# Five PSUM banks, VectorE scaling and ten constant products at the beginning of a two-layer trunk

## The chip, the core and the metric

The kernel runs on one NeuronCore of a Trainium2 chip. The metric is the device time of one execution in microseconds (us); lower is better. The core has TensorE (matrix products, with results in eight PSUM banks of 128 x 512 float32), VectorE, ScalarE and GpSimd for element-wise work, and SyncE, which issues the transfers between DRAM and SBUF. Each engine works through its own queue in order, and engines wait for each other by semaphores.

## What is computed

The reference is a trunk of two layers over a sequence of 1024 frames of 1024 channels. Layer 0 mixes in time by RWKV-7, layer 1 by a diagonal complex state space (S5). A squared-ReLU MLP follows each mixer, and a layer norm follows each of the four parts. The change touches the first part, the projections of the RWKV mixer:

```python
def rwkv7_time_mix(x, mu, w0, w1, w2, a0, a1, a2, g1, g2, k_k, k_a, r_k,
                   wr, wk, wv, wo, lnx_g, lnx_b):
    xx = jnp.pad(x, ((0, 0), (1, 0), (0, 0)))[:, :-1] - x
    xr = x + xx * mu[0]
    xw = x + xx * mu[1]
    xk = x + xx * mu[2]
    xv = x + xx * mu[3]
    xa = x + xx * mu[4]
    xg = x + xx * mu[5]
    r = xr @ wr
    w_pre = (w0 + jnp.tanh(xw @ w1) @ w2).astype(f32)
    decay = jnp.exp(-jnp.exp(-jax.nn.softplus(-w_pre) - 0.5))
    k = xk @ wk
    v = xv @ wv
    a = jax.nn.sigmoid(a0 + (xa @ a1) @ a2)
    g = jax.nn.sigmoid(xg @ g1) @ g2
    ...
    _, o = lax.scan(step, s0, seq_in)
    ...
    return (o.astype(x.dtype) * g) @ wo
```

## The kernel before

Channels lie on the 128 partitions in 8 tiles (KT = 8), frames along the free axis in two halves of 512 (H = 0 and 1). A product in near-float32 precision is made of three fast passes: `split` (L191, L192) lets ScalarE cast a tile to a high part and VectorE subtract it, which gives the low part; `mm3` then issues high x high, high x low and low x high (`mmb`, L256). A product over all 1024 channels is thus 24 matmuls into one PSUM bank.

`rwkv_proj(0)` computes the projections of the first half. It loads the eight `xs` tiles, with the first two weight tiles of `wa1` (list `first`) behind the first of them (L330, L322). `xo` are the split `xs` tiles; `xm` are the mixed ones for `wk` (`mixes(2)`), whose instructions are ranked early (MIXR = 100). The small projections do not mix the input. `scaled` (L383 on) multiplies the weights by `mu` or `1 - mu` instead, on GpSimd (L389), each half of the tile's 128 columns by its own vector; it splits them and takes the product with `xo`. `shifted` adds the two products, one of them a frame later. So come, in program order: `shifted("wa1")` and `gate_a` (two banks each), `gate_c` (one bank for the product with `g1c`, copied out at L427, and one for the products with the constant `pick`, L429 and L430). Then `rates(n)` (two banks, evicted at L467) and `square("wk", ...)` (one bank, evicted at L493) alternate for n = 0 to 3, and four `square("wr", ...)` follow. There the generator yields for the first time.

Every dense product asks `psd()` for its bank, which goes in turn through the list `banks[0]`. That list is `narrow`, three times the pool `pd`, which has three banks. The other PSUM pools are `pl` (one bank), `pa` (two, for the recurrence) and `pc` (two, tag "c"). `kbtrans` of the recurrence writes its transposes into `pc` (L689).

`core` (L870) takes the first step of `rwkv_proj(0)`, then issues `elem(0)`, which reads the stored projections back (`lda`, `ldsg`, `ldk`, `ldr`, L589) and prepares the first unit of the recurrence, `amat` and `invert`, and then the rest of the projections at the lowest urgency. Eight units of the recurrence follow, with the second half's projections among them. The program order isn't the order on the engines: a planner sorts each engine's instructions ahead of time by rank and by estimated times, and assigns the buffers of the pools; at run time each queue is fixed.

Of the kernel before, what the change touches and what calls it, by code (L numbers as in the profile page):

```python
# [30 lines left out]
LNG = (1, 3, 5)  # L31
LNT = (2, 5)
TB = 2
LN2R = 99000
PAUSE = 8
PRE = 6
# [43 lines left out]
def trunk(ctx, tc, A):  # L80
    nc = tc.nc
    V, S, G, PE, SP = nc.vector, nc.scalar, nc.gpsimd, nc.tensor, nc.sync
# [9 lines left out]
    pc = ctx.enter_context(tc.tile_pool(name="pc", bufs=2, space=PSUM))  # L92

    @contextmanager
    def rank(base):

        keep = tc.cur_priority
        tc.cur_priority = base
        yield
        tc.cur_priority = keep  # L100
# [5 lines left out]
    ident = cp.tile([128, 128], F32, name="ident")  # L106
# [83 lines left out]
    def split(src, hi, lo, e=None):  # L190
        S.copy(hi, src)  # L191
        op = (e or V).tensor_sub(lo, src, hi.bitcast(F32))  # L192
        if e is None or e is V:
            behind(op)
            weave(op, pace_[0])
# [62 lines left out]
    def mm3(p, whi, wlo, xh, xl, first, last):  # L258
        mmb(p, whi, xh, start=first, stop=False)
        mmb(p, whi, xl, start=False, stop=False)  # L260
        mmb(p, wlo, xh, start=False, stop=last)
# [33 lines left out]
    narrow = [(pd, "d")] * 3  # L295
    wide = narrow + [(pa, "a")] * 2 + [(pc, "c")] * 2
    banks, nb = [narrow], [0]

    def psd():
        pool, tag = banks[0][nb[0] % len(banks[0])]  # L300
        nb[0] += 1
        return pool.tile([128, HT], F32, tag=tag, name="d")
# [13 lines left out]
    def rwkv_proj(H):  # L316
# [3 lines left out]
        def wraw(nm, k0):  # L320
            w = wp.tile([128, 4, 128], F32, tag="wraw", name="wsc", bufs=4)
            SP.dma_start(w, A[nm][:, k0 : k0 + 4])  # L322
            return w

        first = []
        for k in range(KT):
            t = ap.tile([128, HT + 1], F32, tag="xs", name="xs", bufs=8)
            if H == 0:
                V.memset(t[:, 0:1], 0.0)
                SP.dma_start(t[:, 1:], A["xT"][k * 128 : (k + 1) * 128, 0:HT])  # L330
                if k == 0:
                    first = [wraw("wa1", k0) for k0 in (0, 4)]
# [49 lines left out]
        def scaled(nm, parts):  # L382
            p = psd()  # L383
            n = 128 // len(parts)
            for k0 in range(0, KT, 4):
                w = first.pop(0) if first else wraw(nm, k0)
                for q, m in enumerate(parts):
                    wq = w[:, :, q * n : q * n + n]
                    G.tensor_mul(wq, wq, m[:, k0 : k0 + 4].unsqueeze(2).broadcast_to([128, 4, n]))  # L389
                hi = wp.tile([128, 4, 128], F32R, tag="whi", name="whi")  # L390
                lo = wp.tile([128, 4, 128], F32R, tag="wlo", name="wlo")
                split(w, hi, lo)
                for k in range(4):
                    mm3(p, hi[:, k], lo[:, k], xo[k0 + k][0], xo[k0 + k][1], k0 + k == 0, k0 + k == KT - 1)
            return p
# [262 lines left out]
    def amat(D):  # L658

        shp = [128, 2, NC, NP, 2, L]  # L660
        if D.m in (1, 3, 5):
            at = ap.tile(shp, F32, tag="q", name="AT2", bufs=1)
        else:
            at = kp.tile(shp, F32, tag="AT", name="AT", bufs=1)
        D.at = at
        for j in range(2):
            for c2 in range(2):
                pp = [pa.tile([128, 2, 2, 128], F32, tag="a", name="pA") for h in range(2)]
                prods = []
                for cc in range(2):  # L670
                    for i in range(2):
                        for h in (1, 0):
                            hs = slice(64 * h, 64 * h + 64)
                            u = 4 * i + 2 * c2 + cc
                            prods.append(PE.matmul(pp[h][:, cc, i], D.KB[j][hs, u].rearrange("p j l -> p (j l)"),
                                                   D.AR[j][hs, u].rearrange("p j l -> p (j l)"), start=True, stop=True))
                inorder(prods)
                for h in range(2):
                    V.tensor_mul(at[:, h, 2 * c2 : 2 * c2 + 2, 2 * j : 2 * j + 2].rearrange("p c i j l -> p c i (j l)"),
                                 pp[h], amask.rearrange("p u j l -> p u (j l)").unsqueeze(1).broadcast_to([128, 2, 2, 128]))  # L680

    def kbtrans(D):
        D.kbt = {}
        for j in range(2):
            for c2 in range(2):
                p = pc.tile([128, 2, 2, 128], F32, tag="c", name="pT")
                for cc in range(2):
                    for i in range(2):
                        PE.transpose(p[:, cc, i], D.KB[j][:, 4 * i + 2 * c2 + cc].rearrange("p j l -> p (j l)"), ident)  # L689
                t = kp.tile([128, 2, 2, 128], F32, tag="kbt", name="kbt", bufs=KTB)  # L690
                S.copy(t, p)
                D.kbt[j, c2] = t
# [171 lines left out]
    def run(gen):  # L864
        for _ in gen:
            pass
# [3 lines left out]
    def core():  # L870

        pg = rwkv_proj(0)
        next(pg)
        bulk.clear()
        with rank(3000):
            cur = elem(0)
        with rank(5000):
            amat(cur)
            invert(cur)
        with rank(100000):  # L880
            run(pg)
        last = None
        for m in range(8):
            if m == PB:
                with rank(100000):
                    run(rwkv_proj(1))
            if m == W0B:

                with rank(WO0R):
                    first_out.append(wo(0))  # L890
                with rank(LN1R):
                    first_out.append(layer_norm(first_out[0], 0, 0, True, True))
            base = m * 10000
            with rank(base + RK[0]):
                kbtrans(cur)
            nxt = None
            if m < 7:
                with rank(base + RK[1]):
                    nxt = elem(m + 1)
            if last and m in GB:  # L900
                with rank(base + RK[2]):
                    gnorm(last, 1)
            with rank(base):
                chain(cur, 0)
            if last and m not in GB:
                with rank(base + RK[2]):
                    gnorm(last, 1)
            if nxt and m < 6:
                with rank(base + RK[3]):
                    amat(nxt)  # L910
            with rank(base + RK[4]):
                chain(cur, 1)
            with rank(base + RK[5]):
                gnorm(cur, 0)
            if nxt:
                with rank(base + RK[6]):
                    if m == 6:
                        amat(nxt)
                    invert(nxt)
            last, cur = cur, nxt  # L920
        with rank(base + 8000):
            gnorm(last, 1)
# [40 lines left out]
    def layer_norm(h, gi, H, split_out=True, by_pe=False):  # L963
        ops = []
        for _ in norm_steps(h, gi, H, split_out, ops, by_pe):
            pass
        return ops
# [136 lines left out]
    def wo(H):  # L1104
        t0 = H * HT
        ys = yload(H)
        hs = []
        for n in range(KT):
            p = psd()
            dense(p, wload(A["wo"][n], KT, 128), ys)  # L1110
            h = htile(H)
            SP.dma_start(h, A["xT"][n * 128 : (n + 1) * 128, t0 : t0 + HT])
            V.scalar_tensor_tensor(h, h, ALPHA, p, op0=ALU.mult, op1=ALU.add)
            hs.append(h)
        return hs
# [463 lines left out]
    def store(H, h):  # L1579
        for k in range(KT):  # L1580
            S.dma_start(A["out"][k * 128 : (k + 1) * 128, H * HT : (H + 1) * HT], h[k])

    core()
    kctx.close()
    sp = ctx.enter_context(tc.tile_pool(name="sp", bufs=1))
# [6 lines left out]
    def first_steps(steps, base):  # L1592
        with rank(base):
            next(steps)
            woven.append([steps, tc.cur_priority])
# [46 lines left out]
    def first_half():  # L1642
        yield from norm_steps(hA, 2, 0, True, xo)
        for k in range(4):
            t = jp.tile([128, HT], F32, tag="ql", name="t1r", bufs=6)
            S.copy(t, hA[k])
            t1.append(t)
            t = jp.tile([128, HT], F32, tag="qh", name="t3r", bufs=6)
            G.tensor_sub(t, hA[k + 4], hA[k])
            t3.append(t)  # L1650
            d = [jp.tile([128, HT], F32R, tag="t1", name="t3", bufs=8) for _ in range(2)]
            split(t, *d)
            tops[2].append(d)
            yield 1

    first_steps(first_half(), LN2R)
    glu(hB, ys)
# [49 lines left out]
    for c in range(2):  # L1707
        db(tuple(range(JB - TB, JB)), False, slice(256 * c, 256 * c + 256), keep)
        if c == 0:
# [77 lines left out]
```

## Time and profile before

| | |
|---|---|
| median of 3 runs | 2559.0 us (2554.05 to 2559.45) |
| profiled execution | 2551.81 us |
| its span in the trace | 2550.0 us |
| instructions | 42959 |
| mean granted TensorE clock | 0.973 |

The trace holds one execution. "Busy" is the time in which an engine had an instruction in work, so the overlapping matmuls make TensorE's figure generous. A row of the timeline has start, duration, engine, line, operation, output and inputs, shapes and count. In brackets stands how long the engine was idle before, and what ended that. A row of the waits has the total, the number and the longest. A row of the stretches has, for each engine, busy time and instructions, then the clock granted to TensorE, the mean share of the 16 DMA engines, and GB/s.

### The profile page before, as it was taken

Reading aid. Unit: us, or ns where it says so; the run is one execution under the profiler, and the core shown is the slowest. Engines: PE = TensorE matmul, PEld = TensorE weight load, DVE = VectorE, ACT = ScalarE, POOL = GpSimd, SP = SyncE. Lnnn points to the kernel's source line nnn. Section 1 sums busy time; section 2 is a strip of 40 time slices with the busy share of each in tenths; the row PEclk is TensorE's granted clock in tenths of the full one; section 3 lists DMA queues with packets and bytes.
Section 4 is the critical chain, followed back from the end, with each engine's and each line's share of the span. In section 5 each row is a group of like instructions: output and inputs, shape, how many; then the busy total and the mean of one; then the engine's idle time right before and its main releaser. Section 6 shows DMA issues by size and latency. Waiting matters only on the chain.

```text
span 2550.0 us, 42959 instructions
## 1 busy us (share of the span) xinstructions
PE 2464.4 (97%) x16300; PEld 2008.4 (79%) x16300; DVE 1713.5 (67%) x3307; ACT 1217.8 (48%) x2197; POOL 413.2 (16%) x336
## 2 busy tenths in 40 slices
PE   7999999999899999999999999999999999999998
PEld 5778777797678788877788887887878888888887
DVE  7467787777786665897666476676666555556555
ACT  7556676544454443345644534344565333333434
POOL 3121323321311101011000000100232111111101
PEclk9999989999789999999999999999999999999999
DMA  4865556663212323444456566244352111111233
GB/s 164 281 229 190 182 176 196 209 183 124 65 56 88 95 89 104 165 120 137 120 162 194 173 227 218 95 158 171 105 185 67 48 52 54 50 54 46 81 117 118
DMA packets 217679, 340.60 MB, mean 134 GB/s; under 512 B 21249, under 2 KB 81793, under 8 KB 217473
## 3 DMA queue, kind: packets, MB, share of 16 engines
q1 hardware_dynamic: 216320, 335.77, 41.7%
q8 instruction: 128, 2.10, 0.3%
q10 hardware_dynamic: 1152, 2.10, 0.2%
q14 instruction: 79, 0.64, 0.1%
HBM read 267.53 MB, written 70.25 MB: 132 GB/s over the span
## 4 chain that ended last, share of the span: by engine, by line
PE 55%; DVE 2%; ACT 1%; DMA 1%; POOL 0%; issue 0%; ACTq 0%; DVEq 0%
PE d L256 41%; PE d L1213 10%; PE pk L1445 1%; PE pu L1484 1%; PE pbu L1496 1%; PE py L1556 1%; PE py L1548 0%; PE pu L1477 0%; PE pyt L1566 0%; DVE oBl L192 0%; POOL sq L1008 0%; PE pb L1461 0%; DMA tb<-tB 0%; DVE t1r L1683 0%; PE pq L1016 0%
## 5 line engine op out<-in xcount | busy, mean ns | idle before, releaser
L191 ACT CAST whi<-wraw 128x512 fp32r<-128x512 f32 x424 | 261.9, 620 | 440.6 <-PE d L256 348.2
L192 DVE TENSOR_TENSOR wlo<-wraw,whi 128x512 fp32r<-128x512 f32 x424 | 311.9, 738 | 224.0 <-ACT whi L191 216.5
L256 PE MATMUL d<-qbuf,whi 128*128 128x512 f32 x1152 | 364.6, 397 | 5.5 <-ACT qbuf L191 4.1
L256 PE MATMUL d<-oAh,whi 128*128 128x512 f32 (+1 forms) x752 | 302.6, 407 | 8.1 <-ACT ev L493 4.1
L256 PE MATMUL d<-oAl,whi 128*128 128x512 f32 (+1 forms) x752 | 300.5, 402 | 1.6 <-DVE oAl L192 1.0
L256 PE MATMUL d<-oAh,wlo 128*128 128x512 f32 (+1 forms) x752 | 298.9, 400 | 0.0
L256 PEld LDWEIGHTS d<-qbuf,whi 128*128 128x128 f32 x1152 | 213.8, 189 | 54.9 <-ACT qbuf L191 5.0
L256 PE MATMUL d<-qbuf,wlo 128*128 128x512 f32 x576 | 223.8, 394 | 0.0
L256 PE MATMUL d<-oBh,whi 128*128 128x512 f32 x496 | 195.6, 395 | 0.0
L256 PE MATMUL d<-oBh,wlo 128*128 128x512 f32 x496 | 195.0, 394 | 0.0
L256 PE MATMUL d<-oBl,whi 128*128 128x512 f32 x496 | 193.8, 391 | 0.0
L256 PEld LDWEIGHTS d<-oAh,whi 128*128 128x128 f32 (+1 forms) x752 | 143.0, 192 | 45.5 <-ACT ev L493 5.5
L256 PEld LDWEIGHTS d<-oAl,whi 128*128 128x128 f32 (+1 forms) x752 | 143.2, 192 | 32.0 <-DVE oAl L192 1.3
L256 PEld LDWEIGHTS d<-oAh,wlo 128*128 128x128 f32 (+1 forms) x752 | 142.8, 191 | 31.1 <-issue 1.0
L256 PE MATMUL d<-qh,whi 128*128 128x512 f32 x416 | 164.0, 394 | 0.0
L256 PE MATMUL d<-qh,wlo 128*128 128x512 f32 x416 | 163.1, 392 | 0.0
L256 PE MATMUL d<-ql,whi 128*128 128x512 f32 x416 | 161.6, 389 | 0.0
L256 PEld LDWEIGHTS d<-qbuf,wlo 128*128 128x128 f32 x576 | 108.8, 189 | 23.3 <-issue 0.2
L256 PEld LDWEIGHTS d<-oBh,wlo 128*128 128x128 f32 x496 | 93.1, 188 | 21.4 <-issue 0.6
L256 PEld LDWEIGHTS d<-oBl,whi 128*128 128x128 f32 x496 | 93.1, 188 | 21.4 <-issue 0.7
L256 PEld LDWEIGHTS d<-oBh,whi 128*128 128x128 f32 x496 | 93.2, 188 | 19.7 <-issue 0.5
L1272 DVE TENSOR_TENSOR hA<-hA,d 128x512 f32<-128x512 f32 x104 | 71.3, 686 | 47.2 <-PE d L256 47.2
(496 smaller groups left out, 5229.8 us busy)
## 6 DMA issues: line engine op xcount, KB each, us to landing
wraw<-in_mw_dram SPq DMA_DIRECT2D x356, 256.0 KB, 2.7
wlo<-low SPq DMA_DIRECT2D x92, 256.0 KB, 2.9
wraw<-in_glu_dram SPq DMA_DIRECT2D x64, 256.0 KB, 2.7
low<-wlo SPq DMA_DIRECT2D x52, 256.0 KB, 3.7
raw<-in_mw_dram SPq DMA_DIRECT2D x52, 256.0 KB, 2.7
wraw<-in_wk_dram SPq DMA_DIRECT2D x32, 256.0 KB, 3.4
wraw<-in_wr_dram SPq DMA_DIRECT2D x32, 256.0 KB, 4.4
wraw<-in_wv_dram SPq DMA_DIRECT2D x32, 256.0 KB, 4.9
```

The costliest lines, as they stand in the source:

```text
L191: S.copy(hi, src)
L192: op = (e or V).tensor_sub(lo, src, hi.bitcast(F32))
L256: bulk.append((PE.matmul(p, w, x, **kw).ins, x.shape[-1]))
L1213: PE.matmul(p, w[:, k], x, start=not add and k + j == 0, stop=k == 3 and j == 2, skip_group_check=True)
L1272: V.tensor_add(z, z, p)
L1445: PE.matmul(p[64 * par : 64 * par + 16, g2], bb[ps_, ri, 4 * f + g2], ca[ps_, g2, ri, 0:8].rearrange("p t c -> p (t c)"), start=ri == 0, s ...
L1484: PE.matmul(p[64 * (1 - e) : 64 * (1 - e) + 64, g], u1[j][:, g].rearrange("p s c -> p (s c)"), sel[:, e], start=True, stop=True)
L1496: PE.matmul(p[qs, ri, g2], tb[:, g2, ri, qs], u[:, 2 * g2 + par], start=True, stop=True)
L1556: prods.append(PE.matmul(pp[par][64 * j : 64 * j + 64, g2], hs[f][qs, ri, g2], tcm[qs, g2, ri], start=False, stop=ri == 1, skip_group_chec ...
```

## The change

There are three parts. While both preloaded weight tiles are still in the list `first`, `scaled` issues ten products of `ident` with itself into the first 128 columns of its bank, ahead of the real products, whose first pass overwrites them. For that same step the scaling runs on VectorE in place of GpSimd. And `core` sets the list of banks to `narrow` and two banks of `pc` up to the first yield of `rwkv_proj(0)`, and back to `narrow` after it.

```diff
+WARM = 10
...
             p = psd()
             n = 128 // len(parts)
             for k0 in range(0, KT, 4):
+                begin = len(first) == 2
+                if begin:
+                    for _ in range(WARM):
+                        PE.matmul(p[:, 0:128], ident, ident, start=True, stop=True)
                 w = first.pop(0) if first else wraw(nm, k0)
                 for q, m in enumerate(parts):
                     wq = w[:, :, q * n : q * n + n]
-                    G.tensor_mul(wq, wq, m[:, k0 : k0 + 4].unsqueeze(2).broadcast_to([128, 4, n]))
+                    (V if begin else G).tensor_mul(wq, wq, m[:, k0 : k0 + 4].unsqueeze(2).broadcast_to([128, 4, n]))
...
         pg = rwkv_proj(0)
+        banks[0] = narrow + [(pc, "c")] * 2
         next(pg)
+        banks[0] = narrow
         bulk.clear()
```

## The prediction

> **What bounds the kernel now.** I read the engine totals first, then the idle time of TensorE in the first 100 us by what ended it, then the same stretch cut at those waits.
>
> ```profile
> PE 2464.4 (97%) x16300; PEld 2008.4 (79%) x16300; DVE 1713.5 (67%) x3307; ACT 1217.8 (48%) x2197; POOL 413.2 (16%) x336
> ...
> PE d L256 <- ACT whi L191: 8.9, 1, 8.9
> PE d L256 <- ACT ev L493: 4.1, 1, 4.1
> PE d L429 <- ACT e L427: 2.0, 1, 2.0
> PE d L256 <- DVE oS L192: 1.8, 2, 1.1
> PE d L256 <- DVE wlo L192: 1.7, 1, 1.7
> ...
> 9.00:22.30 13.30, 9.69 (x27) 5.14 (x27) 13.02 (x15) 11.26 (x21) 8.65 (x8) 1.00 0.37 139
> 22.30:44.10 21.80, 21.78 (x94) 17.56 (x94) 19.04 (x31) 15.68 (x28) 8.71 (x7) 1.00 0.44 141
> ...
> 46.10:70.50 24.40, 24.24 (x100) 16.48 (x100) 12.81 (x19) 20.38 (x36) 2.58 (x2) 0.93 0.59 205
> ...
> 74.60:100.00 25.40, 25.40 (x104) 20.68 (x105) 8.31 (x12) 10.18 (x18) 0.00 (x0) 0.93 0.92 319
> 100.00:160.00 60.00, 60.00 (x315) 46.90 (x314) 33.38 (x51) 32.80 (x62) 9.91 (x8) 1.00 0.78 263
> ```
>
> The columns of the last rows are the stretch, its length, the busy time of PE, weight load, VectorE, ScalarE and GpSimd, then granted clock, DMA share and GB/s. TensorE is busy 97% of the span: a microsecond of its idle time won early counts in full, as long as the next stage can also come earlier. In the first 100 us it is idle 18.5 us, in five kinds. From 9 to 22.3 us VectorE is busy 13.02 of 13.30: there TensorE waits for split operands, not for banks or its clock. From 22.3 to 44.1 it has no gap. Then come two waits: 2.0 us for the first gate's copy (L427), and 4.1 us for an eviction of `square` (L493), which is a wait for a PSUM bank. From 74.6 to 160 it is full again.
>
> **First part: VectorE scales.** The words say two tiles. By the diff, `begin` holds only while both preloaded tiles are still in `first`, so it is one tile, k0 = 0, whose two halves are scaled.
>
> ```profile
> 6.17 3.16 POOL L389 TENSOR_TENSOR wsc<-wsc,mum 128x256 f32<-128x256 f32 x4 [3.06 <-DMA wsc<-in_wa_dram]
> ...
> 8.22 0.62 ACT L191 CAST whi<-wsc 128x512 fp32r<-128x512 f32 x1 [1.62 <-POOL wsc L389]
> ...
> 6.01 0.69 DVE L192 TENSOR_TENSOR oS<-xs,oS 128x512 fp32r<-128x512 f32 x1 [2.17 <-ACT oS L191]
> 6.63 1.08 DVE L355 SCALAR_TENSOR_TENSOR m<-xs,pv,m 128x512 f32<-128x512 f32 x1
> 8.87 1.01 DVE L192 TENSOR_TENSOR wlo<-wsc,whi 128x512 fp32r<-128x512 f32 x1 [1.16 <-ACT whi L191]
> ```
>
> GpSimd takes 3.16/4 = 0.79 us for a half. No row has the product on VectorE; the nearest is the 128x512 subtraction at 0.68 us (row of 71.25, below), so half as many elements cost between 0.34 and, at a full row's price, 0.68 us. I take 0.4 each, 0.8 for two, near the first since the work is by element. VectorE now waits for the tile's transfer itself, with the `xs` subtractions queued behind and TensorE waiting for those; but the tile has landed by 6.17, when VectorE is still in the subtraction of 6.01. Behind the subtraction at 6.01 the products would run 6.7 to 7.5 and the cast would start at 7.5 rather than 8.22: 0.7 us gained. Behind the multiply-add of 6.63 they would run 7.7 to 8.5: 0.3 us lost. VectorE is idle 1.16 us before 8.87, which hides the 0.8 us; without that cover all 0.8 us would be lost, since every later operand of this stage queues behind it. GpSimd is then also finished sooner, and the subtraction of 1.01 us may fall to 0.68: 0.33 gained. I take **0.5 us**, ends -0.3 and 1.0.
>
> **Second part: ten products of constants.** They need `ident` alone and an empty bank, and stand ahead of the first real product.
>
> ```profile
> 1.07 0.29 POOL masks.py:199 TENSOR_SCALAR_AFFINE_SELECT ident<-ident 128x128 f32<-128x128 f32 x1
> ...
> 8.89 1.22 PE L256 MATMUL d<-oS,whi 128*128 128x512 f32 x2 [8.89 <-ACT whi L191]
> ...
> 14.18 0.40 PE L256 MATMUL d<-oS,whi 128*128 128x512 f32 x1
> 15.31 0.50 PE L256 MATMUL d<-oS,whi 128*128 128x512 f32 x1 [0.74 <-DVE oS L192]
> ...
> 22.29 0.50 PE L256 MATMUL d<-oS,wlo 128*128 128x512 f32 x1 [1.70 <-DVE wlo L192]
> ...
> 112.19 0.66 PE L619 MATMUL pn<-ident,sq 128*128 128x128 f32 x4
> 112.69 0.95 PE L646 MATMUL pb<-rksel,kf 128*128 128x2 f32 x8
> ```
>
> Four 128x128 products start and hand on in 112.69 - 112.19 = 0.50 us, 0.125 each. The full-precision product of L429 leaves two records for one call (its row stands below), so ten are 20 passes: 2.5 us, or 5.0 at half speed. From 1.36 us they end at 3.9 to 6.4, before any real product can start: they cost nothing, and are not in anyone's way. Do they help? The first 13 real products take 5.29 us from 8.89 to 14.18 against 12 x 0.236 = 2.8 at the later pace of 24 in 5.66 us (below). But right behind, TensorE idles 0.74 us, and later 1.70 us, for VectorE's results, so an earlier arrival there only lengthens those waits. I take **0**, ends 0 and 2.5. The Trainium skill, "TensorE: Matmul & The Clock Gate", Part 1 (The HAM clock gate), says that about 3.4 us of sustained activity lifts the array from half to full clock, and that an idle window of about 3.4 us drops it again. By it ten products may warm the clock, but a pause until 8 us may cool it; this trace is stricter, since the idle 2.03 us at 44.1 was already followed by slow products (0.57 us each in the next fence) while the idle 1.70 us before 22.29 was not.
>
> **Third part: five banks.** Calls of `psd` before the first yield are, in order: 4 for `wa1` and `g1a`, 1 for `g1c`, 1 for the gate's pick products, then 3 for each pair of `rates` and `square`. In turn over three banks each `square` gets the bank of the `square` before it.
>
> ```profile
> 46.11 1.13 PE L429 MATMUL d<-e,pick 128*128 128x512 f32 x2 [2.03 <-ACT e L427]
> ...
> 48.66 1.22 PE L256 MATMUL d<-stash,whi 64*128 64x512 f32 x4
> ...
> 50.24 0.72 PE L256 MATMUL d<-oAh,whi 128*128 128x512 f32 x1
> ...
> 56.13 0.73 PE L256 MATMUL d<-stash,whi 64*128 64x512 f32 x4
> ...
> 57.17 0.50 PE L256 MATMUL d<-oAh,whi 128*128 128x512 f32 x1
> ...
> 62.83 0.74 PE L256 MATMUL d<-stash,whi 64*128 64x512 f32 x4
> ...
> 74.58 0.79 PE L256 MATMUL d<-oAh,whi 128*128 128x512 f32 x1 [4.08 <-ACT ev L493]
> ...
> 81.76 0.63 PE L256 MATMUL d<-oS,whi 128*128 128x512 f32 x2
> ...
> 293.97 1.13 PE L429 MATMUL d<-e,pick 128*128 128x512 f32 x2
> ...
> 295.79 0.28 PE L434 MATMUL d<-carry_p,pick 128*128 128x1 f32 x2
> ```
>
> At 70.5 us the fourth `wk` square (call 17 from 0) wants the bank of the third (call 14). With five banks it takes the one of call 12, a `rates` result long evicted. The 4.08 us go, and with them the slow clock behind them: this square took 81.76 - 74.58 = 7.18 us against 62.83 - 57.17 = 5.66 for the second, so 1.52 more. Sum **5.6 us**.
>
> At 44.1 us the pick products wait for a copy of the gate's bank. Three banks can't hold the gate, the pick and the two of `rates`; five hold these and the first `wk` square, whose operands are ready, so the planner can put `rates` and `wk` into the gap. That saves 2.03 us, and the slow clock: pick products 2.55 us against 1.82 at 293.97, the first `rates` 1.58 against 1.04, the first square 5.89 against 5.66, together 1.50. Sum **3.5 us**, or 0 if the pick keeps its place.
>
> The two borrowed banks belong to `kbtrans`, which needs the recurrence's operands (100.59 us, below). Their last borrower is the second `wr` square (call 19), over at 81.76 + 2 x 5.66 = 93, so the loan costs nothing; without that gap, the recurrence would wait for one eviction, 0.57 us.
>
> What is late next is the supply.
>
> ```profile
> 48.77 0.60 ACT L436 ACTIVATE hd<-d 128x512 f32<-128x512 f32 x1 [2.71 <-PE d L430]
> ...
> 72.64 0.91 ACT L607 ACTIVATE kk<-ldk,pv 128x256 f32<-128x256 f32 x2 [1.94 <-DMA ldk<-s_k]
> ...
> 73.96 0.57 ACT L493 COPY ev<-d 128x512 f32<-128x512 f32 x1
> ...
> 71.25 0.68 DVE L192 TENSOR_TENSOR wlo<-wraw,whi 128x512 fp32r<-128x512 f32 x1
> ```
>
> Without both waits the fourth `wk` square starts at 43.6 + (24.4 - 1.5) = 66.5 and needs its second weight tile 2.8 us on, at 69.3; that tile's low part is now done at 71.93, so 2.6 us late. ScalarE, which casts ahead of it, is busy 20.38 of 24.40 us but idle 2.71 for the pick, which also moves, so it can give much of that back. I subtract **1.4 us**, ends 0 and 4 (the upper adds ScalarE's wait of 1.94 us for the transfer of `ldk`, behind which the next weight casts queue). DMA, 0.92 of its engines from 74.6 to 100, is near its limit too, but TensorE isn't idle there today.
>
> **Sum.** 0.5 + 0 + 5.6 + 3.5 - 1.4 = 8.2 us. The profiled execution, 2551.81 us with a span of 2550.0, would be 2543.6; it lies 7.2 us under the median of the runs shown, 2559.0, so against that median the forecast is **2550.8**.
>
> **Rivals.** What becomes of 8 us later is read here:
>
> ```profile
> 103.86 0.95 PE L611 MATMUL pss<-hsel,sq 128*128 128x2 f32 x8
> ...
> 100.59 0.69 DVE L636 TENSOR_TENSOR AR<-ldr,E 128x512 f32<-128x512 f32 x1 [3.71 <-DMA ldr<-s_r]
> ...
> 600.00:700.00 100.00, 88.08 (x870) 72.69 (x869) 73.69 (x178) 40.26 (x79) 23.25 (x19) 0.83 0.21 68
> ```
>
> 1. *Only the bank wait goes*; the pick still waits. For it: the order is fixed by a planner whose times I can't see. Gain 0.5 + 5.6 - 0.2 = 5.9 us, 2553.
> 2. *The warm clock pays*, by the rule above: if operands come sooner than I think, up to 2.5 us more, 2548. Against it: VectorE's 13.02 of 13.30 us.
> 3. *Supply or recurrence eats it*: casts, transfers or a new order of the recurrence leave 0 to 4 us, 2557.
> 4. *Slower.* The recurrence of layer 0 lives on projection products that fill TensorE's gaps; they run out at 600 to 700 us (88.08 busy, clock 0.83). If the projections come 8.2 us sooner and the recurrence doesn't, as much filler is missing there. Idle alone gives back the gain; in four pieces of 2 us, each with the 1.5 us of slow clock seen at 44 us, it adds 6 us: 2565. It decides when the recurrence starts less than about 3.5 us earlier (s = 6(8.2 - s)/8.2). Against it: its first products, at 103.86, and the operand at 100.59 hang on stored `wr` squares, which the same products bring forward.
> 5. *The change does nothing*: another condition stood behind L493's wait, and the same wait follows it. Against it: ScalarE's eviction at 73.96 and the product at 74.58 fit closely. 2559.
>
> **Chances.** Forecast 0.42; rivals 1 to 5: 0.13, 0.08, 0.20, 0.10, 0.07. About 0.2%, 5.1 us, is what a measurement of this kernel can tell from no change. Faster by more: 0.42 + 0.08 + most of rival 1 (0.10) = 0.60. Slower: 0.10. The same: 0.30. The range runs from 2542 (first and second part at their upper ends and no supply loss: 12.6 us, and the 4 to 5 us by which the runs shown lie under their median) to 2562 (rivals 3 and 5 with half as much above); rival 4 and a luckier order of the recurrence are left out, 0.2 together.
>
> **What would show it.** Right: no wait for L493 at 70 us; products of `rates` or `wk` ahead of the pick; the 4th `wk` square of about 5.7 us; the first `pss` product near 96 us; constant products over before 6.5 us, and still an idle wait for VectorE before 22 us. Wrong: a wait for L191 or L192 of over 3 us in 60 to 80 us (supply), a `pss` start after 100 us, or idle time in 300 to 800 us that differs from today's by more than 5 us, which no term above contains.

## The result and the profile after

| | before | after |
|---|---|---|
| median (range, runs) | 2558.7 us (2554.05 to 2559.45, 5) | 2540.7 us (2537.8 to 2541.43, 5) |
| ratio of the times | 1 | 0.9935 [0.9923, 0.9948] |
| profiled execution | 2551.81 us | 2540.41 us |
| its span | 2550.0 us | 2538.7 us |

The change makes the kernel 0.65% faster, 16.6 us by the ratio; the two profiled executions differ by 11.4 us. The forecast was 2550.8, the range 2542 to 2562. The direction holds, the gain is twice the 8.2 us of the sum, and the time lies 1.3 us under the range (by the ratio, 2542.4 us against the 2559.0 of the forecast, it lies at its very end). TensorE's line in the engine totals of the changed kernel tells little:

```profile
PE 2468.8 (97%) x16320; PEld 2012.3 (79%) x16320; DVE 1712.5 (67%) x3309; ACT 1216.7 (48%) x2197; POOL 410.1 (16%) x334
```

It has 20 more matmuls, the ten constant products of two passes each. What answers to the waits shown of before are the waits of TensorE in the first 100 us of the changed kernel (who waits, for whom, total us, times, longest; the diff moves the lines of before down by one to seven: L493 is now L498, L467 is L472, L427 is L432; in the kernels without constants these numbers are three lower):

```profile
PE d L257 <- ACT whi L192: 1.5, 1, 1.5
PE d L257 <- ACT ev L472: 1.5, 1, 1.5
...
PE d L257 <- ACT oS L192: 1.4, 2, 1.1
PE d L257 <- ACT ev L498: 0.4, 1, 0.4
PE d L257 <- DVE oS L193: 0.2, 1, 0.2
```

The 4.1 us for the `square` eviction are gone (0.4 are left, for another one at 95 us), the 2.0 us for the gate's copy are gone, and so are the 1.7 us for `wlo`. Two kinds are new: 1.5 us for L472, the eviction of `rates`, and 1.4 us in two pieces for ScalarE's cast of `xs` tiles, the longer because the second tile's transfer landed only at 8.69 us. The same stretches as before, in the changed kernel (stretch, length, busy time of PE, weight load, VectorE, ScalarE and GpSimd, granted clock, DMA share, GB/s):

```profile
0.00:9.00 9.00, 5.27 (x23) 4.28 (x23) 5.48 (x35) 3.46 (x5) 2.44 (x13) 0.94 0.72 226
9.00:22.30 13.30, 12.46 (x35) 8.78 (x36) 12.84 (x14) 10.56 (x20) 9.00 (x9) 0.65 0.41 150
...
46.10:70.50 24.40, 22.95 (x105) 16.86 (x104) 13.38 (x19) 19.84 (x36) 2.56 (x2) 1.00 0.73 250
74.60:100.00 25.40, 25.00 (x117) 20.29 (x116) 11.17 (x16) 11.35 (x21) 3.77 (x2) 1.00 0.94 320
```

Read the counts behind PE: from 9 to 22.3 us 35 matmuls in place of 27, from 74.6 to 100 us 117 in place of 104. In the second row TensorE was busy 9.69 us and is busy 12.46, at a granted clock of 0.65: it now has operands there and lacks pace.

The timeline of TensorE in the changed kernel shows the new order:

```profile
4.79 0.61 PE L390 MATMUL d<-ident 128*128 128x128 f32 x4
6.94 0.73 PE L257 MATMUL d<-oS,whi 128*128 128x512 f32 x2 [1.55 <-ACT whi L192]
...
9.36 1.52 PE L257 MATMUL d<-oS,whi 128*128 128x512 f32 x2 [1.13 <-ACT oS L192]
...
18.26 0.40 PE L257 MATMUL d<-oS,wlo 128*128 128x512 f32 x1
...
40.95 0.40 PE L257 MATMUL d<-oS,wlo 128*128 128x512 f32 x1
41.52 0.50 PE L257 MATMUL d<-oAh,whi 128*128 128x512 f32 x1 [0.17 <-ACT e L406]
...
47.11 1.02 PE L434 MATMUL d<-e,pick 128*128 128x512 f32 x2
...
48.92 0.73 PE L257 MATMUL d<-stash,whi 64*128 64x512 f32 x4
...
52.08 0.50 PE L257 MATMUL d<-oAh,whi 128*128 128x512 f32 x1 [1.45 <-ACT ev L472]
...
65.19 0.50 PE L257 MATMUL d<-oAh,whi 128*128 128x512 f32 x1
...
70.77 0.63 PE L257 MATMUL d<-oS,whi 128*128 128x512 f32 x2
```

The constants end at 5.4 us. The product with `g1c` ends 2.7 us earlier (its last pass starts at 40.95, before at 43.69). The first `wk` square stands in the old gap, from 41.52 to the pick products at 47.11. These take 1.81 us to the first `rates` at 48.92, where they took 2.55. The fourth `wk` square takes 70.77 - 65.19 = 5.58 us, where it took 7.18 after its wait. The first `wr` product starts at 70.77 in place of 81.76: 11.0 us earlier.

**Where the rest came from.** I cut both traces at the same instructions: the first `pA` product of the recurrence (135.17 us before, 124.63 after) and the first `pk` product of layer 1 (1118.2 and 1100.4). Up to the first cut the changed kernel gains 10.5 us, between the cuts 7.3 more, and after the second it loses 6.5. The stretches say what kind of time this is. Before, with its first cut at 290 us:

```profile
290.00:1118.20 828.20, 793.87 (x6510) 646.46 (x6506) 611.20 (x1437) 418.45 (x791) 172.80 (x134) 0.94 0.42 131
1118.20:1950.00 831.80, 819.53 (x5357) 662.90 (x5357) 560.52 (x918) 401.48 (x705) 77.81 (x54) 1.00 0.50 157
1950.00:2550.00 600.00, 587.34 (x2676) 485.06 (x2674) 340.64 (x541) 224.48 (x385) 90.25 (x71) 0.99 0.22 68
```

After, cut where the matched instructions stand (11.2 us earlier at the first):

```profile
278.80:1100.40 821.60, 791.70 (x6517) 643.32 (x6515) 611.61 (x1437) 418.22 (x791) 171.74 (x134) 0.94 0.42 132
1100.40:1937.00 836.60, 824.15 (x5357) 666.61 (x5357) 560.20 (x917) 401.95 (x705) 77.44 (x53) 0.99 0.49 156
1937.00:2538.70 601.70, 588.94 (x2676) 485.97 (x2674) 338.88 (x541) 224.47 (x385) 90.36 (x71) 0.99 0.22 68
```

In the first stretch, the recurrence of layer 0 with projections as filler, the changed kernel has 821.60 - 791.70 = 29.9 us of idle time against 34.3, and 2.2 us less busy time. From `pk` on the instructions of TensorE stand in the same order in both kernels (5357 and 2676 of them), and yet the changed one needs 4.8 and 1.7 us more, mostly as busy time: the same products at a slower pace. One place is near 1750 us. Before, a pause, then a product of the next stage 1.87 us behind:

```profile
1750.97 0.71 PE L1566 MATMUL pyt<-ident,y 64*128 64x64 f32 x8 [1.74 <-DVE yg L1568]
...
1752.84 0.50 PE L256 MATMUL d<-oAh,wlo 128*128 128x512 f32 x1
```

After, the same instructions with a pause 0.38 us longer, and 3.28 us between the same two:

```profile
1734.95 1.03 PE L1573 MATMUL pyt<-ident,y 64*128 64x64 f32 x8 [2.12 <-DVE yg L1575]
...
1738.23 0.62 PE L257 MATMUL d<-oAh,wlo 128*128 128x512 f32 x1
```

So the two traces hold three things: a gain at the beginning, a gain in the recurrence, and a difference after 1100 us that the change can't have made by another order on TensorE. The experiments take them apart.

### The profile page after: what moved, and what is told of

It reads as the page before. It is cut to its first block, busy times and chain, and to the rows that moved or that the text cites. A ratio compares the mean times of both kernels' runs of the same rounds, so it can differ in the third digit from the quotient of the medians.

```text
span 2538.7 us, 42992 instructions
## 1 busy us (share of the span) xinstructions
PE 2468.8 (97%) x16320; PEld 2012.3 (79%) x16320; DVE 1712.5 (67%) x3309; ACT 1216.7 (48%) x2197; POOL 410.1 (16%) x334
## 4 chain that ended last, share of the span: by engine, by line
PE 71%; DVE 7%; DMA 2%; ACT 1%; issue 1%; POOL 0%; ACTq 0%; DVEq 0%
PE d L257 53%; PE d L1220 10%; PE pA L680 1%; PE pk L1452 1%; DMA yl<-s_y 1%; DVE wlo L193 1%; PE pq L944 1%; PE pu L1491 0%; PE pU L798 0%; PE py L1563 0%; PE pO L809 0%; PE pbu L1503 0%; PE pO L807 0%; PE pR L788 0%; DVE oBl L193 0%
## 5 line engine op out<-in xcount | busy, mean ns | idle before, releaser
L257 PEld LDWEIGHTS d<-oBh,whi 128*128 128x128 f32 x496 | 93.2, 188 | 19.7 <-issue 0.5
```

The costliest lines, as they stand in the source:

```text
L257: bulk.append((PE.matmul(p, w, x, **kw).ins, x.shape[-1]))
```

## The experiments

The theories were: the gain is that of the banks; it needs the scaling too; the constants pay or don't; and a good part comes from the order of the recurrence that the planner happens to find, or from the phase of TensorE's clock. The runs come from several chips, so times of different kernels are compared by their ratios to the kernel before on the same chip.

**The constants: none, 14, 20.** With these counts every engine has the instructions of the changed kernel in the same order, but for the constants.

```diff
-                if begin:
-                    for _ in range(WARM):
-                        PE.matmul(p[:, 0:128], ident, ident, start=True, stop=True)
```

```diff
-WARM = 10
+WARM = 14
```

```diff
-WARM = 10
+WARM = 20
```

> The changed kernel without its ten constant products; all engines' orders are otherwise the same. In the changed kernel the array ran at half pace from 9.4 to 17.9 us. Theory A (forecast: the constant products are worth nothing, operands bind): the first wk product starts at 41.5 us as with them, within 0.5 us, and the time stays within 3 us of 2540.7. Theory B (they warm the array): the first three real products at 0.43 us each in place of 0.23, the first wk product 0.5 to 2.5 us later. Theory C (they bring the slow stretch on, since the pause after them drops the clock): full pace from about 11 us, 4 us after the first product as in the kernel before, and the first wk product 1 to 2.5 us earlier.

> The changed kernel with 14 constant products in place of 10, all orders the same: at 0.4 us each they end at 7.0 us, where the first real product starts, so the pause of 1.55 us is gone. Theory A: no change over 0.5 us at the first wk product (41.5 us). Theories B and C, if that pause drops the clock: full pace through 9 to 18 us and the first wk product 1.5 to 2.5 us earlier. If the array is slow all the same, the pause after the first three real products (1.13 us) or something else sets the clock.

> The changed kernel with 20 constant products, all orders the same: they end at 7.5 us if the clock comes up on the way and at 9.4 us if it does not. Theory A: the first real product 0.5 to 2.5 us later, the first wk product at 41.5 us within 0.5 us, since operands bind. Theories B and C: full pace from the first real product on, the first wk product 1.5 to 2.5 us earlier.

Measured: 2538.5 us without (0.9940 [0.9923, 0.9957]), 2535.3 with 14 (0.9924 [0.9909, 0.9939]), 2538.1 with 20 (0.9940 [0.9925, 0.9955]), all against the kernel before and all in the interval of the changed kernel. The first `wr` product starts at 70.44, 70.55 and 70.24 us; with ten it was 70.77. The traces say why a warm array buys nothing. Without constants:

```profile
7.40 1.22 PE L257 MATMUL d<-oS,whi 128*128 128x512 f32 x2 [7.40 <-ACT whi L192]
...
15.25 0.39 PE L257 MATMUL d<-oS,wlo 128*128 128x512 f32 x1
...
19.23 0.50 PE L257 MATMUL d<-oS,wlo 128*128 128x512 f32 x1 [0.58 <-DVE wlo L193]
```

With 20:

```profile
8.51 0.71 PE L257 MATMUL d<-oS,whi 128*128 128x512 f32 x2
...
12.33 0.50 PE L257 MATMUL d<-oS,whi 128*128 128x512 f32 x1 [0.54 <-DVE oS L193]
...
15.79 0.50 PE L257 MATMUL d<-oS,whi 128*128 128x512 f32 x1 [0.96 <-DVE oS L193]
...
19.28 0.50 PE L257 MATMUL d<-oS,wlo 128*128 128x512 f32 x1 [0.58 <-DVE wlo L193]
```

With 20 the real products run at full pace from the first, and wait for VectorE three times instead; without, they start at half pace and reach the full one at 15.25. They arrive at 19.23 and 19.28 us at the same operand, after the same wait of 0.58 us. VectorE sets the end of this stage in both, and the pace only decides how TensorE spends the time until then. With ten and 14 the products at half pace come some 0.3 us too late to wait: the last `g1c` product starts at 40.95 and 40.98 us, against 40.65 without and 40.69 with 20.

**Each part alone.** The constants alone, the banks alone and the scaling alone, each an edit of the kernel before:

```diff
+                begin = len(first) == 2
+                if begin:
+                    for _ in range(WARM):
+                        PE.matmul(p[:, 0:128], ident, ident, start=True, stop=True)
```

```diff
+        banks[0] = narrow + [(pc, "c")] * 2
         next(pg)
+        banks[0] = narrow
```

```diff
+                begin = len(first) == 2
...
-                    G.tensor_mul(wq, wq, m[:, k0 : k0 + 4].unsqueeze(2).broadcast_to([128, 4, n]))
+                    (V if begin else G).tensor_mul(wq, wq, m[:, k0 : k0 + 4].unsqueeze(2).broadcast_to([128, 4, n]))
```

> The kernel before with the ten constant products alone, all orders as before. Theory A: the product after the wait at 22.29 us starts there within 0.3 us, and so does everything behind it; the time is that of before within 0.1%. Theory B: the first real products at full pace, but the same time, as VectorE binds here. Theory C: the slow stretch moves to later than 13 us and the first 25 products end up to 1.5 us later; the time is 0 to 2 us longer.

> The kernel before with the five banks alone. Three times are read: the first wr product (81.8 us before, 70.8 with the whole change), the first pA product of the recurrence (135.2 before, 124.6 after), and the whole. Theory A (the forecast's steps: both waits and their slow stretches go, 9.1 us, less 0 to 4 for supply): first wr product at 72.7 to 76.7, first pA 7 to 9 us earlier, the whole 5 to 12 us shorter. Theory D (the recurrence's new order, not the beginning, makes most of the gain): the beginning as in A, but the whole within 3 us of before or over 15 us shorter. Theory E (the bank waits only uncover a supply that VectorE's scaling feeds): first wr product later than 77.

> The kernel before with VectorE scaling the first tile alone. Theory A (forecast: 0.5 us, ends -0.3 and 1.0): the product behind the wait at 22.29 us and all behind it 0.5 us earlier; first wr product at 81.3. Theory F (the first tile's way through GpSimd held up the whole operand stage): the g1c products end 2.7 us earlier as with the whole change, the waits of 2 and 4 us stay, first wr product at 79, first pA 2 to 3 us earlier, the whole 0 to 6 us shorter.

| | time, us | ratio [95%] | last `g1c` product | first `wr` | first `pA` |
|---|---|---|---|---|---|
| before | | 1 | 43.69 | 81.76 | 135.17 |
| constants alone | 2562.6 | 1.0036 [1.0023, 1.0049] | 44.72 | 82.61 | 135.98 |
| banks alone | 2542.8 | 0.9946 [0.9926, 0.9967] | 43.06 | 72.41 | 125.78 |
| scaling alone | 2557.2 | 1.0002 [0.9988, 1.0017] | 40.97 | 81.92 | 135.32 |
| all three | 2540.7 | 0.9935 [0.9923, 0.9948] | 40.95 | 70.77 | 124.63 |

The banks carry the gain: alone they bring the first `wr` product 9.4 us forward, 0.6 of it there already at the end of `g1c`, since the first weight tile came earlier in this execution. The scaling alone gains 2.7 us up to the end of `g1c`, and has lost all of it by the end of the pick products, as TensorE's timeline shows for the kernel with the scaling alone:

```profile
40.97 0.39 PE L257 MATMUL d<-oS,wlo 128*128 128x512 f32 x1
45.22 2.07 PE L431 MATMUL d<-e,pick 128*128 128x512 f32 x2 [3.86 <-ACT e L429]
```

With three banks nothing stands ahead of the pick. ScalarE, with casts ahead in its queue, reaches the gate's copy at 44.60 us, only 0.9 us sooner than before (45.48), so the wait there grows from 2.03 to 3.86 us, and the slow products behind it come too. Only with the banks does the scaling count: 11.0 us together at the first `wr`, against 9.4 and -0.2 alone.

The constants alone are a surprise, 0.36% slower in six runs, though the order on every engine is that of before and the first `pA` comes only 0.8 us later. (With the banks and the scaling, ten constants cost nothing that the intervals show: 0.9935 with, 0.9940 without.) Their trace, cut as above, for the kernel with the constants alone:

```profile
288.90:1120.70 831.80, 794.55 (x6508) 646.99 (x6506) 612.97 (x1437) 419.15 (x793) 173.41 (x134) 0.94 0.42 130
1120.70:1957.20 836.50, 823.31 (x5357) 665.77 (x5357) 560.95 (x916) 401.70 (x705) 76.92 (x53) 0.99 0.50 156
1957.20:2558.40 601.20, 589.70 (x2676) 487.06 (x2674) 340.45 (x541) 224.49 (x385) 90.29 (x71) 0.99 0.22 68
```

Set beside the changed kernel, this is the fairer partner: the last two stretches agree within 0.1 and 0.5 us, and the changed kernel gains 10.1 us up to the first cut and 10.2 in the recurrence, 19.7 in all. So the 6.5 us that the changed kernel seemed to lose after 1100 us are a lucky end of the execution of before that was profiled. The two also show how far executions of one order can lie apart: 3.6, 4.7 and 1.2 us more over the three stretches than the same order took before, and 1.1 less ahead of them. Why all six executions lie high, no run shows.

**Both tiles on VectorE, and seven banks.** Without constants; the first scales the second preloaded tile on VectorE too, the second lends the two banks of `pa` as well:

```diff
                 begin = len(first) == 2
+                early = len(first) > 0
...
-                    (V if begin else G).tensor_mul(
+                    (V if early else G).tensor_mul(
```

```diff
-        banks[0] = narrow + [(pc, "c")] * 2
+        banks[0] = narrow + [(pa, "a")] * 2 + [(pc, "c")] * 2
```

> The changed kernel without the constant products, and with both preloaded tiles scaled on VectorE, as the change's words have it; to be held against the run without constant products (first wr product 70.4 us). Theory A: VectorE gains 0.76 us of work in the stage that it binds, GpSimd loses 1.2: first wr product 0 to 0.8 us later. Theory F (GpSimd is the late one, and slows VectorE while it runs): 0 to 1 us earlier.

> The changed kernel without the constant products and with seven banks (the two of pa as well) in the beginning; to be held against the run without constant products. If the new wait of 1.45 us for an eviction (L472, at 50.6 us) is one for a bank, it goes: first wr product 1 to 1.5 us earlier, at about 69.2, unless weight casts take its place. First pA 0 to 1.5 us earlier; later if the recurrence, whose pool is borrowed, now waits. The whole within 5 us of 2538.5.

Both tiles: 2538.7 us, 0.9932 [0.9911, 0.9953], first `wr` at 70.75. That is what one tile gives. Seven banks: 2549.3 us, 0.9971 [0.9956, 0.9987]. The new wait for L472 is gone and the first `wr` starts at 69.97, but at 98 us TensorE waits for an operand of the recurrence, as the timeline of the kernel with seven banks shows:

```profile
97.78 1.57 PE L648 MATMUL pb<-rksel,kf 128*128 128x2 f32 x8 [3.32 <-POOL kf L645]
99.21 0.78 PE L257 MATMUL d<-oAh,whi 128*128 128x512 f32 x1
99.78 0.63 PE L257 MATMUL d<-oAl,whi 128*128 128x512 f32 x1
```

GpSimd computes `kf` from 96.02 us on, after the transfer of the stored `r`. That is no later than in the changed kernel (95.92), where `pb` stands at 102.15: here the planner put `pb` ahead of the dense products, and these then run at 0.43 us each. The first `pA` still comes 12.0 us earlier than before; what this kernel loses, it loses behind it.

**The same beginning with another order: 24 and 28 constants.** With 24 and 28 the planner sorts the engines differently.

```diff
-WARM = 10
+WARM = 24
```

```diff
-WARM = 10
+WARM = 28
```

> The whole change with 24 constant products. What the products do at the beginning was seen to be nothing; here the planner's estimate of their length makes it order all engines differently from some 25 instructions on (with 20 the orders were still those of the changed kernel). So this has the same beginning and another order of the recurrence. Theory D (the 5 to 8 us by which the whole changed kernel gained more than its beginning belong to the order the planner happened to choose): first wr product at 70 to 72, first pA at 123 to 126, but the whole anywhere between 2530 and 2550, over 4 us from 2540. Theory G (any kernel that begins 10 us earlier gains 16): the whole within 4 us of 2540.

> As the run before, with 28 constant products and once more another order. Same readings: first wr product at 70 to 73, first pA at 123 to 127; theory D: the whole over 4 us from that of 24 or from 2540; theory G: within 4 us of both, beyond what the beginning itself is later.

Measured: 2546.1 us (0.9953 [0.9937, 0.9969]) and 2539.9 us (0.9935 [0.9920, 0.9950]). The first `pA` starts at 124.90 and 124.37 us, as with ten. So by the ratios one order costs some 5 us against the changed kernel (the intervals still touch), and the other nothing, with one and the same beginning.

**A list of four banks, and one of six,** without constants:

```diff
-        banks[0] = narrow + [(pc, "c")] * 2
+        banks[0] = narrow + [(pc, "c")]
```

```diff
-        banks[0] = narrow + [(pc, "c")] * 2
+        banks[0] = narrow + [(pc, "c")] * 2 + [(pl, "l")]
```

> The changed kernel without the constant products and with four banks. By the rotation, the fourth wk square (call 17) then takes the bank of call 13, a rates result, so the wait of 4 us at its start is gone as with five; the first wk square (call 8) takes the bank of the gate (call 4) and must wait for the same copy as the pick products, while the first rates can go ahead. Expected: the wait for the copy comes down from 3.9 us (VectorE's scaling alone) to 1.5 to 3, first wr product at 72 to 75 against 70.4 with five. If it is at 70.5 or earlier, the order of wk and pick is not what saves the time at 44 us; if it is over 77, four banks do not free the fourth square.

> The changed kernel without the constant products and with six banks: the sixth is the one of pl, which the recurrence's inversion uses later. Seven banks took away the wait of 1.45 us at 51 us but brought a wait of 3.3 us of the recurrence's product pb at 98 us. If the borrowed pool pa was the cause of that, six banks keep the gain (first wr product at 69.3 to 70, first pA at 122.5 to 124) and the whole is 2533 to 2540; if the earlier projections themselves shift the order so, the wait at 98 us is here too and the whole is 2545 to 2552.

The list of four doesn't leave the core with four banks: the pool `pc` has two and hands them out in turn, so calls 3 and 7 get one each, and five are in use in another order. The bank wait at 70 us is gone. The first `wr` starts at 78.62 us, later than I had expected. TensorE's timeline of the kernel with the list of four:

```profile
44.75 0.50 PE L257 MATMUL d<-oAh,whi 128*128 128x512 f32 x1 [2.69 <-ACT whi L192]
...
45.32 1.14 PE L431 MATMUL d<-e,pick 128*128 128x512 f32 x2
...
49.67 0.79 PE L257 MATMUL d<-oAh,whi 128*128 128x512 f32 x1
```

The first `wk` square gets the gate's bank (call 4) and starts behind the pick, at 49.67 us. What waits 2.69 us ahead of the pick is the second square, for the cast of its weights; two of its passes stand there. This wait and the slow products up to 53 us are most of the loss. And yet the whole takes 2540.7 us (0.9926 [0.9906, 0.9945]), the same as the kernel without constants (0.9940). Six banks: first `wr` at 69.27, first `pA` at 116.32, and then TensorE waits at 124 us:

```profile
123.92 0.53 PE L257 MATMUL d<-oAh,whi 128*128 128x512 f32 x1 [3.27 <-ACT ev L495]
```

In all 2542.2 us (0.9942 [0.9929, 0.9954]): no gain over five. Neither reading of the expectation fits, as the first `pA` comes 7.5 us earlier than without constants and with five, and the whole does not.

**All traces in one table,** each against the trace of before, in us: up to the first `pA`, from there to the first `pk`, and from there to the end, each to within 0.2 us. (Banks alone is left out, as its order moves the first `pk`.)

| | to `pA` | `pA` to `pk` | `pk` to end |
|---|---|---|---|
| changed kernel (10 constants) | -10.5 | -7.3 | +6.5 |
| 0 constants | -11.3 | -3.6 | +3.7 |
| 14 constants | -10.5 | -9.5 | +4.1 |
| 20 constants | -11.3 | -3.7 | +5.4 |
| constants alone | +0.8 | +1.7 | +5.9 |
| scaling alone | +0.2 | -1.8 | +1.9 |
| both tiles | -11.0 | -5.0 | +7.2 |
| 24 constants | -10.3 | +3.3 | +6.1 |
| 28 constants | -10.8 | -7.9 | +2.8 |
| list of four banks | -3.2 | -11.4 | +4.2 |
| six banks | -18.9 | +3.4 | +4.9 |
| seven banks | -12.0 | +6.9 | +5.0 |

The last column is positive in every row: the trace of before is the odd one there. The middle column moves by 18 us between kernels, and doesn't follow the first: the kernel with the least gain at the beginning of those with more banks gains most behind it. The first four rows share one order and still differ by 5.9 us there; that is what executions of one order can differ by, and the table can't say whether the clock or the transfers make it. (Both tiles on VectorE leave TensorE's order the same too, and lie among them.) Their mean is -6.0, while the two rows with the order of before (itself, 0, and the constants alone, +1.7) lie outside their spread. What in the order of the recurrence makes the 6 us I haven't found, and how much of it belongs to the order and how much to the execution stays open. So the gain of the beginning is shown at the first `pA`; that it reaches the end in full is not, as the list of four gains 3.2 us there and no less in all. No kernel beat the changed one by more than the intervals allow. The one without constants is as fast and shorter.

## Why the prediction was right and where it failed

- **Bank wait at 70.5 us, 5.6 us: right.** The wait is gone, and the square took 5.58 us, close to the 5.66 of the second square of before. With the list of four it goes too, as the call numbers say.
- **Pick wait at 44.1 us, 3.5 us: right,** by the mechanism named: the first `wk` square fills the gap, and the slow products behind it are gone. It needs a bank for that square that is neither the gate's nor the pick's: with three banks (scaling alone) the wait grew to 3.86, and with the list of four, which gives it the gate's, another of 2.69 us stood in its place. (The 0.57 us each that the prediction took as slow don't show it: the row of 293.97 has the same 1.13 us for two. The 2.55 us against 1.82 do.)
- **Supply, -1.4 us: right in size by luck, wrong in place.** Nothing waited for a cast of a weight tile at 70 us. The loss was the 1.45 us at 52 us, where the second `wk` square wants the bank of the first `rates`. ScalarE evicts that at 51.36, behind two instructions of the gate and two of the mixing, as its timeline in the changed kernel shows:

```profile
49.02 0.60 ACT L441 ACTIVATE hd<-d 128x512 f32<-128x512 f32 x1 [1.32 <-PE d L435]
49.52 1.32 ACT L359 ACTIVATE m<-xs,pv 128x512 f32<-128x512 f32 x2
50.75 0.71 ACT L417 ACTIVATE hd<-hd,half 128x512 f32<-128x512 f32 x1
51.36 0.67 ACT L472 ACTIVATE ev<-d,pvh 128x512 f32<-128x512 f32 x1
```

- **Constants, 0: right** in the kernel with the banks and the scaling. The reason given (VectorE sets the end of the stage) holds without constants and with 20, where TensorE waits 0.58 us for it. In the changed kernel the wait for VectorE before 22 us, promised as a sign, was 0.25 us: its products ran at half pace up to 18 us and came some 0.3 us too late for the later one.
- **VectorE scales, 0.5 us: mis-sized.** It measured 2.7 us at the end of `g1c`, 2.1 against the kernel with the banks alone, whose first weight tile also came early. The earlier transfer isn't the cause: with seven banks the first `xs` tile landed later than before (5.67 against 5.36 us), and `g1c` ends at 40.63. The price of an instruction was right; the timeline of VectorE in the changed kernel has it behind the subtraction, as taken, at 0.38 us a half:

```profile
5.48 0.76 DVE L394 TENSOR_TENSOR wsc<-wsc,mum 128x256 f32<-128x256 f32 x2
6.16 0.74 DVE L356 SCALAR_TENSOR_TENSOR m<-xs,pv,m 128x512 f32<-128x512 f32 x1
6.92 0.69 DVE L193 TENSOR_TENSOR wlo<-wsc,whi 128x512 fp32r<-128x512 f32 x1
...
17.95 1.53 DVE L193 TENSOR_TENSOR wlo<-wsc,whi 128x512 fp32r<-128x512 f32 x1
```

  The gain of the first cast was right too: it starts 2.05 us behind the first cast of `xs` in place of 2.86, so 0.8 us. (The low part of 8.87 now starts at 6.92, but 1.14 us of that is an earlier transfer in this execution.) The step that failed took this cast, and at most 0.33 us of a faster subtraction, as the whole gain, with VectorE's queue behind it unchanged. But the planner sorted that queue anew. Before, VectorE came to the third low part, for which TensorE waited until 22.29, at 20.71 us:

```profile
19.26 1.52 DVE L192 TENSOR_TENSOR oAl<-m,oAh 128x512 fp32r<-128x512 f32 x1
20.71 1.52 DVE L192 TENSOR_TENSOR wlo<-wsc,whi 128x512 fp32r<-128x512 f32 x1
```

  It comes to it at 17.95 in the changed kernel. Three subtractions of mixed tiles (`oAl`) stood between the first low part and this one; now two do, in every kernel that scales on VectorE, and the third, 1.45 us at 19.26, follows later. So half of the 2.8 us is a new order, which the term couldn't contain. The waits of TensorE of 0.74, 1.07 and 1.70 us, which the prediction counted as a reason why the constants can't help, are what an earlier VectorE shortens. With the scaling alone they were 0.23, 0.25 and 0.21.
- **The beginning as a whole.** 2.7 + 0 + 5.6 + 3.5 - 1.45 = 10.4 us. The first `wr` product came 11.0 us earlier and the first `pA` 10.5: with the one term mended, the sum closes to 0.6 us.
- **From the profiled execution to the median: not the step that failed.** Adding the 7.2 us by which the execution of before lay under its median is the same as taking 8.2 us off the median 2559.0, and that is right, as that distance was mostly luck behind 1100 us (4.8 us by the mean of the table's last column). Executions of the kernel before spread from 2543.8 to 2565.6 us in 23 runs on one chip. Profile against profile the forecast was 2543.6 and 2540.4 came; that this looks closer is luck, as there 7.3 us of the recurrence, which the sum hasn't, and 6.5 us behind it nearly cancel.
- **The recurrence, no term: the missing piece.** Rival 4 bounded only a loss there, and a luckier order was put outside the range. The recurrence did come forward with the beginning (10.5 of the 11.0 us at the first `wr`), so rival 4 had no ground, and idle time from 300 to 800 us fell from 33.1 to 29.4 us, within the 5 us allowed. But the stretch from `pA` to `pk` gave 6.0 us more on average over the four traces of this order. The beginning's mean of 10.9 in these four and this 6.0 make 16.9, and the ratio says 16.6. This closes only if the whole of the last column is luck of the one execution of before, so it is an account and not a proof.
- **Rivals 1, 2, 3 and 5** fell with these rows: the pick no longer waits, constants up to 20 leave the first `wr` between 70.24 and 70.77 us, the gain is there at the first `pA`, and the waits named did go.
- **The sign "first `pss` near 96 us"** was a bad one: the planner put it at 79.0, far ahead of what it feeds. The first `pA` was the instruction to watch.

## What to carry to other kernels

A bank that comes free late is paid twice on TensorE, once as the wait and once as slow products behind it, and a few microseconds won ahead of such a wait are worth nothing until it goes: the scaling alone was worth 0, and with the banks 1.6 us at the first `wr`. Where a planner sorts the whole kernel, an edit of the first 100 us also draws a new order for the next 1000; keep some 10 us of such luck, of both signs, in the range (here from -11.4 to +6.9 us). Take a forecast gain off the median, not off the one execution that was profiled: the two lay 7.2 us apart here, nearly the whole forecast. Compare several traces of one order, and cut them at the same instructions.

## What was not expected of the hardware

- Pauses of some 2 us were followed by slow products, and not each time: 2.12 us near 1735 us in the changed kernel was, 1.74 us near 1751 us in the kernel before was not, nor was 1.45 us at 52 us. The closest pair: with the constants alone the products behind a wait of 1.69 us at 21.74 us follow each other at 0.43 us, and with the banks alone, behind the same wait at 21.66 us, at 0.23. The length of one pause doesn't decide it; where the pause falls seems to matter, which no run isolates. The Trainium skill, "TensorE: Matmul & The Clock Gate", Part 1, puts the window at about 3.4 us of idle time. These traces don't agree with that as a bound on one pause.
- A slow stretch can be long: in the changed kernel, products follow each other at 0.43 us from 11.5 to 18 us with no pause over 0.25 us, though ten constants had run before. Without constants the full pace came at 15.25 us, 7.9 after the first product.
- The granted clock in the rows doesn't always show it: the stretch from 9 to 22.3 us has 0.65 in the changed kernel and 1.00 in the one before, whose first products were as slow (13 in 5.29 us). The starts of the products show the pace; the column alone doesn't.
- Ten more products at the start of the kernel before, with everything behind them in the same order, cost 0.36% of the whole, some 9 us. In the one trace 0.8 us of it lie at the beginning and 1.7 in the recurrence; the 5.9 us behind stand against the lucky end of the trace of before. Where the rest lies and why all six executions are high stays open.
